# Layer normalization on one core: early rows of the fourth tile on a second queue, and the first tile's statistics in two groups

## Chip, cores, metric

One core of a Trainium2 chip. The metric is the device time of one execution in microseconds (us), smaller is better; executions of this kernel agree within some 0.2%. A profile is one execution recorded by the hardware profiler; its span is 1.6 to 2.0 us shorter than the time of the same execution in the runs here.

## The reference

```python
def setup_inputs():
    batch, seq, dim = 32, 512, 1024
    return {"x": np.random.randn(batch, seq, dim).astype(np.float32), "eps": 1e-5}

def reference(x, eps):
    mean = np.mean(x, axis=-1, keepdims=True)
    var = np.var(x, axis=-1, keepdims=True)
    return ((x - mean) / np.sqrt(var + eps)).astype(np.float32)
```

16384 rows of 1024 floats: 67.1 MB in, 67.1 MB out, and little arithmetic.

## The kernel before

Each of the 128 partitions holds 48 rows of 4 KB, a ring of six tiles of 8 rows. For each tile: a load; `bn_stats` on VectorE (two per row); nine small GpSimd steps that merge the partial statistics; a square root on ScalarE; a reciprocal on VectorE; a product on GpSimd; eight normalising passes on ScalarE, in place; a store. Loads go out on the SyncE queue, stores on the ScalarE queue; the load of tile t waits until tile t-6 is stored.

```python
TILES = (8,) * 15 + (6, 2)
SLOT, SLOTS = 8, 6
HALVES, PARTS = (4, 4), (8,)
# ... first tile: two halves, one on each queue
for n, engine, sem in zip(HALVES, (nc.sync, nc.scalar), (landed[0], later)):
    engine.dma_start(out=ring[:, at+first : at+first+n, :],
                     in_=rows_of(x2, row, K)[:, first : first+n, :]).then_inc(sem, 16)
# ... later tiles, behind the store that frees their place
    dma = nc.sync.dma_start(out=ring[:, at : at+K, :], in_=rows_of(x2, row, K)
                            ).then_inc(landed[t], 16)
    if gone:
        dma._wait_ge(stored[gone[-1]], sixteens(stored, gone[-1]))
# ... VectorE, per tile
    for k in range(K):
        for s in range(NSUB):
            i = nc.vector.bn_stats(...)      # first one waits for the load
    i.then_inc(taken, 1)
    nc.vector.reciprocal(out=rstd[...], in_=std[...])._wait_ge(rooted[t], turn).then_inc(inverse, 1)
# ... GpSimd: nine steps from `taken`, then nmr = -mean * rstd from `inverse`
# ... ScalarE: sqrt, K x activation(Identity, bias=nmr, scale=rstd), then the store
```

## Time and profile before

| | before |
|---|---|
| time, median of 3 runs | 317.88 us (317.74 to 317.92) |
| span of the profile | 315.9 us |
| VectorE, ScalarE, GpSimd busy | 156.8, 153.0, 39.3 us |
| bytes moved, mean rate | 134.24 MB, 425 GB/s |

The engines that compute are idle half the time or more. A packet is what one of the 16 DMA engines moves at a time: a transfer of a whole tile of 8 rows is 128 packets of 32 KB, one for each partition. The row "DMA" of the page gives the share of time for which the 16 DMA engines were busy in each of 40 slices; it and the stretches are shown in the prediction below.

### The profile page before, as it was taken

What the parts mean: (1) busy time and instruction counts of PE and PEld (TensorE: products, weight loads), DVE (VectorE), ACT (ScalarE), POOL (GpSimd) and SP (SyncE); (2) the same over time, 40 slices, a digit from 0 to 9 for tenths busy, and PEclk for the clock granted to TensorE, in tenths of its full rate; (3) what the DMA queues carried; (4) which work ended last, traced back from release to release, by engine and by line L of the source; (5) the groups of instructions that cost most, each with busy time, mean ns of one, the idle gap of its engine ahead of it and who ended that gap; (6) DMA issues with size and microseconds to landing.
All of it is one profiled execution on the core that took longest, in us unless ns stands there. A gap on an engine that the chain in (4) does not pass through costs nothing.

```text
span 315.9 us, 694 instructions
## 1 busy us (share of the span) xinstructions
DVE 156.8 (50%) x274; ACT 153.0 (48%) x146; POOL 39.3 (12%) x174
## 2 busy tenths in 40 slices
DVE  0296595965190752908438093470925619193000
ACT  1006595865925609165190742908338092476600
POOL 0002202022002020020201102011020200203100
DMA  7999999999999999999999999999999999999996
GB/s 292 438 452 411 452 402 407 457 407 461 403 462 415 448 419 444 419 444 431 431 436 427 444 423 440 423 448 415 452 415 456 419 431 442 435 430 427 427 421 288
DMA packets 5043, 134.24 MB, mean 425 GB/s; under 512 B 560, under 2 KB 560, under 8 KB 560
## 3 DMA queue, kind: packets, MB, share of 16 engines
q10 hardware_dynamic: 2592, 69.21, 51.0%
q1 hardware_dynamic: 2448, 65.01, 47.9%
q14 instruction: 3, 0.02, 0.0%
HBM read 67.11 MB, written 67.11 MB: 425 GB/s over the span
## 4 chain that ended last, share of the span: by engine, by line
DMA 61%; DVE 18%; ACT 9%; POOL 4%; issue 2%; ACTq 0%; DVEq 0%; SPq 0%
DMA ring<-in_x_dram 31%; DMA out_dram<-ring 29%; DVE stats L115 17%; ACT ring L210 9%; ACT std L200 1%; POOL dev L173 1%; POOL dev L178 1%; POOL dev L166 0%; POOL dev L171 0%; POOL nmean L162 0%; POOL half L156 0%; POOL half L179 0%; POOL ss L182 0%; DVE rstd L124 0%; POOL nmean L160 0%
## 5 line engine op out<-in xcount | busy, mean ns | idle before, releaser
L115 DVE BATCH_NORM_STATS2 stats<-ring 128x6 f32<-128x512 f32 x256 | 153.5, 678 | 82.2 <-DMA ring<-in_x_dram 81.6
L210 ACT ACTIVATE ring<-ring,nmr,rstd 128x1024 f32<-128x1024 f32 x128 | 146.6, 1227 | 9.3 <-POOL nmr L190 9.3
L200 ACT ACTIVATE std<-ss,eps_t 128x8 f32<-128x8 f32 (+2 forms) x17 | 5.1, 300 | 134.3 <-POOL ss L182 133.9
L156 POOL TENSOR_TENSOR half<-stats 128x16 f32<-128x16 f32 (+2 forms) x17 | 3.9, 232 | 232.9 <-DVE stats L115 232.9
L124 DVE RECIPROCAL rstd<-std 128x8 f32<-128x8 f32 (+2 forms) x17 | 3.4, 200 | 55.4 <-ACT std L200 55.4
L173 POOL TENSOR_SCALAR dev<-dev 128x32 f32<-128x32 f32 (+2 forms) x17 | 5.0, 293 | 1.5
L190 POOL TENSOR_TENSOR nmr<-nmean,rstd 128x8 f32<-128x8 f32 (+2 forms) x17 | 3.5, 203 | 11.9 <-DVE rstd L124 11.9
L178 POOL TENSOR_TENSOR dev<-dev,stats 128x32 f32<-128x32 f32 (+2 forms) x17 | 4.3, 254 | 1.4
L166 POOL TENSOR_TENSOR dev<-stats,nmean 128x32 f32<-128x32 f32 (+2 forms) x17 | 4.1, 239 | 1.4
L171 POOL TENSOR_TENSOR dev<-dev 128x32 f32<-128x32 f32 (+2 forms) x17 | 4.0, 235 | 1.3
L162 POOL TENSOR_SCALAR nmean<-nmean 128x8 f32<-128x8 f32 (+2 forms) x17 | 4.0, 233 | 1.5
L179 POOL TENSOR_TENSOR half<-dev 128x16 f32<-128x16 f32 (+2 forms) x17 | 3.6, 213 | 1.3
L182 POOL TENSOR_TENSOR ss<-half 128x8 f32<-128x8 f32 (+2 forms) x17 | 3.4, 201 | 1.3
L160 POOL TENSOR_TENSOR nmean<-half 128x8 f32<-128x8 f32 (+2 forms) x17 | 3.4, 200 | 1.3
L200 ACT ACT_TABLE_LOAD x1 | 1.3, 1283 | 1.3 <-SPq L52 1.3
L128 DVE MEMSET eps_t<- 128x1 f32 x1 | 0.1, 59 | 1.0 <-SPq L52 1.0
L246 POOL MEMSET const-float32-0.0<- 128x1 f32 x1 | 0.1, 98 | 0.2 <-issue 0.2
L246 POOL MEMSET const-uint8-127<- 128x1 uint8 x1 | 0.1, 102 | 0.0
L246 POOL MEMSET const-bfloat16-1.0<- 128x1 bf16 x1 | 0.1, 101 | 0.0
L246 POOL MEMSET const-float32-1.0<- 128x1 f32 x1 | 0.1, 98 | 0.0
## 6 DMA issues: line engine op xcount, KB each, us to landing
out_dram<-ring ACTq DMA_DIRECT2D x15, 4096.0 KB, 47.4
ring<-in_x_dram SPq DMA_DIRECT2D x14, 4096.0 KB, 44.3
ring<-in_x_dram SPq DMA_DIRECT2D x1, 3072.0 KB, 42.0
out_dram<-ring ACTq DMA_DIRECT2D x1, 3072.0 KB, 17.8
ring<-in_x_dram ACTq DMA_DIRECT2D x1, 2048.0 KB, 12.4
ring<-in_x_dram SPq DMA_DIRECT2D x1, 2048.0 KB, 12.5
ring<-in_x_dram SPq DMA_DIRECT2D x1, 1024.0 KB, 53.7
out_dram<-ring ACTq DMA_DIRECT2D x1, 1024.0 KB, 16.7
```

The lines of the kernel that those rows point to most:

```text
L115: i = nc.vector.bn_stats(out=stats[:, at + k, s, :], in_=ring[:, at + k, s * BN_MAX : (s + 1) * BN_MAX],)
L124: nc.vector.reciprocal(out=rstd[:, at : at + K], in_=std[:, at : at + K])._wait_ge(rooted[t], turn).then_inc(inverse, 1)
L156: g.tensor_tensor(out=h, in0=mean4[:, :, 0:2], in1=mean4[:, :, 2:4], op=ALU.add),
L162: g.tensor_scalar(out=nm, in0=nm, scalar1=-1.0 / H, scalar2=None, op0=ALU.mult),
L166: g.tensor_tensor(out=d, in0=mean4, in1=nm.unsqueeze(2).to_broadcast([P, K, H]), op=ALU.add),
L171: n = gp(g.tensor_mul(out=d, in0=d, in1=d), *n)
L173: g.tensor_scalar(out=d, in0=d, scalar1=float(D // H), scalar2=None, op0=ALU.mult),
L178: n = gp(g.tensor_tensor(out=d, in0=d, in1=m2, op=ALU.add), *n)
L179: n = gp(g.tensor_tensor(out=h, in0=d[:, :, 0:2], in1=d[:, :, 2:4], op=ALU.add), *n)
L190: g.tensor_mul(out=nmr[:, at : at + K], in0=nm, in1=rstd[:, at : at + K]),
L200: nc.scalar.activation(out=std[:, at : at + K], in_=ss[:, at : at + K], func=AF.Sqrt, bias=eps_t[:], scale=1.0 / D,)._wait_ge(*summed[t]). ...
L210: i = nc.scalar.activation(out=ring[:, k, :], in_=ring[:, k, :], func=AF.Identity, bias=nmr[:, k : k + 1], scale=rstd[:, k : k + 1],).then ...
```

## The change

The intent is an earlier start. The first half of tile 0 no longer shares the DMA engines with the second at equal weight, so it lands sooner; each half gets its own chain of statistics, so the first rows are normalised while the second half is still being measured, and the reciprocal of tile 0 becomes a power on GpSimd, so VectorE need not wait for it. Three rows of the fourth tile (index 3) are loaded from the beginning on the ScalarE queue, which has nothing else to do yet. The diff, cut to its core:

```diff
-HALVES, PARTS = (4, 4), (8,)
+HALVES = (4, 4)
+EARLY, AHEAD = 3, 3
+    power = sbuf("power", [P, SLOT])
@@ loads
+    for k in range(AHEAD):
+        load(nc.scalar, EARLY, k, 1, ahead)          # one row each
+        if t == 0:
+            load(nc.sync, t, 0, HALVES[0], landed[t])
+            load(nc.sync, t, HALVES[0], HALVES[1], second)
+            continue
+        first = AHEAD if t == EARLY else 0
+        dma = load(nc.sync, t, first, K - first, landed[t])
@@ VectorE
+        if t == EARLY:
+            nc.vector.wait_ge(ahead, 16 * AHEAD)
+    nc.vector.memset(power[:], -1.0)
+    statistics(0, HALVES[0], landed[0], 16)
+    statistics(HALVES[0], HALVES[1], second, 16)
+    for t in range(1, FIRST):
@@ GpSimd and ScalarE: loops over 18 groups (4, 4, 8, 8, ...) instead of 17 tiles
+        if t:
+            n = inverse, t
+        else:
+            n = gp(g.tensor_tensor(out=rstd[...], in0=std[...], in1=power[:, :K], op=ALU.pow), ...)
```

The store of tile 0 stays one store of 8 rows.

More of the change, by code (lines that the diff above doesn't have):

```diff
@@ L74, in sixteens @@
     def sixteens(sems, t):
-        if sems is stored and t == 0:
-            return 16 * len(PARTS)
         return 16 * sum(1 for s in sems[: t + 1] if s.num == sems[t].num)
@@ L85, in rows_of, with load @@
         return a[row * P : (row + K) * P].rearrange("(p k) d -> p k d", p=P)
-    later = nc.alloc_semaphore("landed_later")
-    K, row, at = plan[0]
-    first = 0
-    for n, engine, sem in zip(HALVES, (nc.sync, nc.scalar), (landed[0], later)):
-        engine.dma_start(
+    groups = []
+    for t, (K, row, at) in enumerate(plan):
+        for n in HALVES if t == 0 else (K,):
+            groups.append((t, at, n))
+            at += n
+    second, ahead = nc.alloc_semaphore("second_half"), nc.alloc_semaphore("ahead")
+    def load(engine, t, first, n, sem):
+        K, row, at = plan[t]
+        return engine.dma_start(
             out=ring[:, at + first : at + first + n, :],
@@ L95 @@
         ).then_inc(sem, 16)
-        first += n
-    assert first == K
-    owner = {r: 0 for r in range(K)}
-    for t, (K, row, at) in list(enumerate(plan))[1:]:
+    for k in range(AHEAD):
+        load(nc.scalar, EARLY, k, 1, ahead)
+    owner = {}
+    for t, (K, row, at) in enumerate(plan):
         gone = sorted({owner[r] for r in range(at, at + K) if r in owner})
@@ L103, with statistics @@
             nc.sync.wait_ge(stored[g], sixteens(stored, g))
-        dma = nc.sync.dma_start(
-            out=ring[:, at : at + K, :], in_=rows_of(x2, row, K)
-        ).then_inc(landed[t], 16)
+        if t == 0:
[4 more added lines that the diff above has]
+        dma = load(nc.sync, t, first, K - first, landed[t])
         if gone:
             dma._wait_ge(stored[gone[-1]], sixteens(stored, gone[-1]))
+    def statistics(at, n, sem, value):
+        for k in range(at, at + n):
+            for s in range(NSUB):
+                i = nc.vector.bn_stats(
+                    out=stats[:, k, s, :],
+                    in_=ring[:, k, s * BN_MAX : (s + 1) * BN_MAX],
+                )
+                if k == at and s == 0:
+                    i._wait_ge(sem, value)
+        i.then_inc(taken, 1)
     def vector(t, arrived, turn):
         K, row, at = plan[t]
-        for k in range(K):
-            for s in range(NSUB):
-                i = nc.vector.bn_stats(
-                    out=stats[:, at + k, s, :],
-                    in_=ring[:, at + k, s * BN_MAX : (s + 1) * BN_MAX],
-                )
-                if k == 0 and s == 0:
-                    i._wait_ge(landed[t], arrived)
-                if t == 0 and k == HALVES[0] and s == 0:
-                    i._wait_ge(later, 16)
-        i.then_inc(taken, 1)
+        if t == EARLY:
+            nc.vector.wait_ge(ahead, 16 * AHEAD)
+        statistics(at, K, landed[t], arrived)
         nc.vector.reciprocal(
@@ L128 @@
     nc.vector.memset(eps_t[:], eps_val)
-    for t in range(FIRST):
+    nc.vector.memset(power[:], -1.0)
+    statistics(0, HALVES[0], landed[0], 16)
+    statistics(HALVES[0], HALVES[1], second, 16)
+    for t in range(1, FIRST):
         vector(t, 16, 1)
@@ L150 @@
     g = nc.gpsimd
-    for t, (K, row, at) in enumerate(plan):
+    for i, (t, at, K) in enumerate(groups):
         parts = stats[:, at : at + K].rearrange("p g s (h c) -> p g (s h) c", h=2)
@@ L157 @@
             taken,
-            t + 1,
+            i + 1,
         )
@@ L187 @@
         )
+        if t:
+            n = inverse, t
+        else:
+            n = gp(
+                g.tensor_tensor(
+                    out=rstd[:, at : at + K],
+                    in0=std[:, at : at + K],
+                    in1=power[:, :K],
+                    op=ALU.pow,
+                ),
+                rooted[t],
+                i + 1,
+            )
         ready.append(
@@ L192 @@
                 ),
-                inverse,
-                t + 1,
+                *n,
             )
         )
-    for t, (K, row, at) in enumerate(plan):
+    for i, (t, at, n) in enumerate(groups):
         nc.scalar.activation(
-            out=std[:, at : at + K],
-            in_=ss[:, at : at + K],
+            out=std[:, at : at + n],
+            in_=ss[:, at : at + n],
             func=AF.Sqrt,
@@ L205 @@
             scale=1.0 / D,
-        )._wait_ge(*summed[t]).then_inc(rooted[t], 1)
-        parts = PARTS if t == 0 else (K,)
-        ends = [sum(parts[: i + 1]) for i in range(len(parts))]
-        for k in range(at, at + K):
-            i = nc.scalar.activation(
+        )._wait_ge(*summed[i]).then_inc(rooted[t], 1)
+        for k in range(at, at + n):
+            a = nc.scalar.activation(
                 out=ring[:, k, :],
@@ L217 @@
             if k == at:
-                i._wait_ge(*ready[t])
-            if k - at + 1 in ends:
-                n = parts[ends.index(k - at + 1)]
-                a = k + 1 - n
-                nc.scalar.dma_start(
-                    out=rows_of(o2, row, K)[:, a - at : a - at + n, :], in_=ring[:, a : a + n, :]
-                )._wait_ge(act, row + k - at + 1).then_inc(stored[t], 16)
+                a._wait_ge(*ready[i])
+        K, row, at = plan[t]
+        if k == at + K - 1:
+            nc.scalar.dma_start(
+                out=rows_of(o2, row, K), in_=ring[:, at : at + K, :]
+            )._wait_ge(act, row + K).then_inc(stored[t], 16)
     for t in range(len(plan)):
```

## The prediction

> **What bounds the kernel now.** I read the views in this order: the page's slices, its DMA queues, the busy time by stretches, the timeline of the first 80 us, and the packet records behind the trace. Arithmetic is idle half of the time (VectorE 156.8 us, ScalarE 153.0 us of 315.9), the transfers never are:
>
> ```profile
> DMA  7999999999999999999999999999999999999996
> DMA packets 5043, 134.24 MB, mean 425 GB/s; under 512 B 560, under 2 KB 560, under 8 KB 560
> q10 hardware_dynamic: 2592, 69.21, 51.0%
> q1 hardware_dynamic: 2448, 65.01, 47.9%
> HBM read 67.11 MB, written 67.11 MB: 425 GB/s over the span
> ```
>
> Only the first and last of the 40 slices are below 9 tenths, and the two queues together take 98.9% of the time of all 16 engines. The bytes are the least possible: x is read once and the output written once. The stretches say the same (columns: the stretch in us, its length, busy us of VectorE, ScalarE and GpSimd with counts, TensorE clock, DMA share, GB/s):
>
> ```profile
> 0.00:4.00 4.00, 0.06 (x1) 1.28 (x1) 0.19 (x4) 1.00 0.53 143
> 4.00:36.00 32.00, 19.25 (x33) 9.46 (x9) 2.32 (x10) 1.00 1.02 441
> 36.00:40.00 4.00, 0.83 (x3) 0.61 (x2) 2.32 (x10) 1.00 1.06 393
> 40.00:280.00 240.00, 129.96 (x226) 129.66 (x124) 30.18 (x130) 1.00 1.00 432
> 280.00:300.00 20.00, 6.66 (x13) 12.03 (x12) 4.32 (x20) 1.00 1.01 433
> 300.00:313.00 13.00, 0.00 (x0) 0.00 (x0) 0.00 (x0) 1.00 0.97 417
> 313.00:315.90 2.90, 0.00 (x0) 0.00 (x0) 0.00 (x0) 1.00 0.18 73
> ```
>
> Loads alone (4 to 36), loads with stores (40 to 280) and stores alone (300 to 313) all run at about the same rate, so it makes no difference to the total which of them the engines do at a moment, as long as they do one.
>
> The view of the chain that ended last could mislead here: it gives 61% to DMA and 18% to VectorE statistics. Its early part does run through VectorE, but the DMA engines were full of later tiles' loads all that while. What the change speeds up is this start:
>
> ```profile
> 13.48 9.59 DVE L115 BATCH_NORM_STATS2 stats<-ring 128x6 f32<-128x512 f32 x16 [12.42 <-DMA ring<-in_x_dram]
> 26.81 9.16 ACT L210 ACTIVATE ring<-ring,nmr,rstd 128x1024 f32<-128x1024 f32 x8 [0.55 <-POOL nmr L190]
> 36.00 0.35 ACTq L222 DMA_DIRECT2D out_dram<-ring  x1
> 298.01 0.34 ACTq L222 DMA_DIRECT2D out_dram<-ring  x1
> ```
>
> The first store is issued at 36.0 us, the last at 298.0, and the last data lands near 314. The store queue therefore still holds some 15 us of work when the last piece of arithmetic is over: the compute path has that much room at the end.
>
> **The packet records** (the trace holds start, size and duration of every packet; no view prints them singly). The median packet takes 309 ns for 8 KB, 611 ns for 16 KB, 912 ns for 24 KB, 1213 ns for 32 KB: about 602 ns per 16 KB and 8 or 9 ns for the packet. One engine's share is 232 packets of 32 KB, 16 of 24 KB, 16 of 16 KB and 16 of 8 KB: 281.4 + 14.6 + 9.8 + 4.9 = 310.7 us. Before it lie 1.9 us to the first packet; the first packet of each engine took about 1290 ns instead of 611 (0.7 us of exposed latency); and around 39 us, as the first store's packets begin, one load packet of each engine took about 1.8 us instead of 1.21 (0.6 us, the 393 GB/s above). Sum 313.9; some 2 us remain for the last completion, the unequal ends of the engines and the final waits, which makes the span of 315.9. The 317.88 us of the unprofiled runs are 2 us more. There is nothing larger than 1 us in this sum that an earlier start of arithmetic could remove.
>
> **What the Trainium skill says.** "DMA: Bandwidth & Descriptors", section "Where 436 GB/s comes from", puts the ceiling of the 16 engines at 435 GB/s; the trace agrees, with 432 over 240 us. The same page, section "Queues, rings and completion order", has each engine alternate between queues packet by packet, whatever their size. The trace agrees: in the mixed stretch packets of both queues are 32 KB and alternate, and a store of 4 MB takes 43 us from issue, mostly queued, with 19.4 us between tiles. This matters for the change: a 4 KB packet on one queue is answered by a 16 or 32 KB one on the other. The section "Issuing engines are not separate DMA queues" says that issuing from several engines saves only issue time (here 0.37 to 0.39 us per issue). "HBM Reference", "Specifications (TRN2)", puts a lone core at about 425 GB/s; the page's mean is 425.
>
> **The change, part by part.**
>
> *Loads.* Removed: the second half of tile 0 from the ScalarE queue. It now follows the first on the SyncE queue, while ScalarE issues three loads of one row (512 KB each, 128 packets of 4 KB); the fourth tile's own load shrinks to five rows (20 KB packets). Bytes are unchanged. Per engine there are 24 more packets, at about 9 ns: 0.2 us; three more completions of 9 ns are nothing. An estimate from the fit: a 4 KB packet takes 0.16 us. A pair of 16 KB and 4 KB is then 0.77 us, a pair of 32 KB and 4 KB 1.37 us. From the first packet at 1.9 us, with 0.9 us for the first latencies, eight pairs bring half one at about 9.5 (before, 13.48), eight more bring half two at 15.7, and eight with tile 1's packets bring tile 1 and the early rows together at 26.7. Tile 1 thus lands when VectorE used to begin on it (26.41).
>
> *Statistics in two groups.* Eight statistics take 4.8 us (half of 9.6): 9.5 to 14.3. The nine GpSimd steps took 2.8 us (23.15 to 25.93), and cost nearly the same for 4 rows as for 8, since they are 0.20 to 0.30 us each: 17.2. Square root 0.3, then a power on GpSimd in place of VectorE's reciprocal (no duration in this trace; as an estimate 0.2 to 0.5), product 0.2: ScalarE begins about 18.1 and ends four rows at 22.7. Group two: 15.7 to 20.5, sum at 23.4, rows 24.3 to 28.9. Extra work is nine GpSimd steps, a product, two powers and one square root, some 4 us, on engines at 12% and 48%. Gain: VectorE is no longer held for 3.2 us by tile 0's reciprocal, and the first store is issued at about 29 instead of 36.
>
> *What 7 us earlier is worth.* From 29 to 36 the engines now carry stores on half their packets, where they carried only loads. About 7 x 0.216 = 1.5 MB moves from the end to the beginning, and as much loading moves later. The load stream ends about 3.5 us later (the last load landed at 288.75), the last store is issued at about 301.5, and the queue then holds 12 us of stores instead of 15. The end does not move. Sum: +0.2 us for small packets, 0 for the earlier store.
>
> *The fourth tile.* With stores beginning at 29, tile 2 lands near 39.6 and tile 3, five rows at about 2.0 us a pair, near 55. VectorE wants tile 3 at about 53. Whole, it would land near 59. The early rows repair a wait that the earlier store makes, but the wait stands beside full DMA.
>
> **Rivals.**
> 1. *The start is on the path, and 7 us (2.2%) come off.* For it: the chain view runs through VectorE and GpSimd from 13.48 to 75 us. Against it: DMA share 1.02 from 4 to 36 us; a chain of waits does not say that the engines were idle. It would give 311, below the 313.9 that the packets need.
> 2. *Half of it, 3.5 us,* if only-store time at the end ran slower than mixed time. The 417 GB/s from 300 to 313 hints at it; but store packets there take 1214 ns against 1213 in the middle, so that is the uneven count of packets at the edge. It would give about 314.5.
> 3. *A new starvation.* The ring holds six tiles; with less loaded ahead, the store queue could run dry in the steady state or at the end. My times have store 0's packets end near 52 and store 1 issued at 49 (the first store's packets came 3.8 us after its issue), so a short dry spell is likely. Loads fill it, so it costs only what a restart of stores costs, up to the 0.6 us seen at 39. At the end store 15 would be issued about 6 us before its predecessors are drained. A real loss needs both queues empty: two more us would give 320.
> 4. *A better ramp:* a 4 KB first packet might hide the first latency. At most 0.7 us: 317.2.
>
> **Range and chances.** 317.88 + 0.2 for packets, and a few hundredths for a possible restart: 318.1. Rival 4 sets the low end, the restart and unlucky ends of the engines the high end: 317.4 to 318.9. Two per cent are 6.4 us; faster by that is excluded by the packet sum, slower needs a starvation that the room of 6 to 12 us speaks against.
>
> **What would show it.** First statistics near 9.5, first store near 29, VectorE's wait for the reciprocal of tile 0 gone, 384 more packets under 8 KB, DMA share 9 tenths in the same 38 slices, last store issued near 301 instead of 298, same end. I am wrong if a stretch between 4 and 313 us shows a rate below 425 GB/s for 20 us, or if the power or the small loads delay the first store beyond 36 us.

## The result, and the profile after

| | before | after |
|---|---|---|
| time, median | 317.87 us (317.74 to 317.92, 4 runs) | 318.42 us (318.31 to 318.82, 4 runs) |
| span of the profile | 315.9 us | 316.7 us |
| first store issued | 36.00 us | 29.64 us |
| last store issued | 298.01 us | 305.72 us |
| last data written (packet records) | 314.24 us | 314.42 us |

The ratio is 1.002 (95% interval 1.0003 to 1.0038): the same within 2%, and a little slower. A ratio here and below is the mean time of one kernel's fast runs over that of the other's of the same rounds, so it is not quite the ratio of the medians quoted.

The page of the changed kernel, its slices and queues:

```profile
DMA  7999999999999999999999999999999999999996
DMA packets 5476, 134.25 MB, mean 424 GB/s; under 512 B 608, under 2 KB 608, under 8 KB 992
q10 hardware_dynamic: 2880, 68.68, 50.4%
q1 hardware_dynamic: 2592, 65.54, 48.5%
```

The same 38 slices are full. The 384 data packets of 4 KB appear under 8 KB (992 less the 608 small ones). Selected lines of the timeline (start, length, engine, line, what, and in brackets the idle time before it with its releaser):

```profile
9.44 4.84 DVE L128 BATCH_NORM_STATS2 stats<-ring 128x6 f32<-128x512 f32 x8 [8.33 <-DMA ring<-in_x_dram]
15.63 4.85 DVE L128 BATCH_NORM_STATS2 stats<-ring 128x6 f32<-128x512 f32 x8 [1.35 <-DMA ring<-in_x_dram]
17.37 1.04 POOL L212 TENSOR_TENSOR rstd<-std,power 128x4 f32<-128x4 f32 x1 [0.41 <-ACT std L232]
26.60 9.59 DVE L128 BATCH_NORM_STATS2 stats<-ring 128x6 f32<-128x512 f32 x16 [6.12 <-DMA ring<-in_x_dram]
29.64 0.35 ACTq L251 DMA_DIRECT2D out_dram<-ring  x1
54.39 9.59 DVE L128 BATCH_NORM_STATS2 stats<-ring 128x6 f32<-128x512 f32 x16 [0.93 <-DMA ring<-in_x_dram]
...
305.72 0.34 ACTq L251 DMA_DIRECT2D out_dram<-ring  x1
```

Everything the change was made for happened: statistics 4 us earlier, the store 6.4 us earlier. And the stretches, in the columns of the prediction:

```profile
4.00:36.00 32.00, 19.09 (x32) 9.75 (x10) 6.39 (x22) 1.00 1.02 424
36.00:40.00 4.00, 0.39 (x2) 0.35 (x2) 2.35 (x10) 1.00 1.01 434
40.00:280.00 240.00, 127.13 (x220) 122.77 (x117) 30.13 (x129) 1.00 1.00 433
300.00:313.00 13.00, 0.17 (x1) 4.77 (x5) 1.33 (x7) 1.00 0.97 417
313.00:316.70 3.70, 0.00 (x0) 0.00 (x0) 0.00 (x0) 1.00 0.23 95
```

The share is 1.0 as before. The 424 of the first line holds what lay at 36 to 40 us before (393 GB/s there): the stall as stores begin (load packets that take longer than usual while the first stores start), now at 31 to 36 us. ScalarE and GpSimd now still work after 300 us, where they had finished: the end of the arithmetic has moved closer to the end of the transfers.

The profiled span grew by 0.73 us. By the packet records, 0.18 us of it lies before the last data is written. The other 0.55 us come after it, in the closing handshake of the engines.

### The profile page after: what moved, and what is told of

The parts are those of the page before. It is cut to its first block, busy times and chain, and to the rows that moved or that the text cites. A ratio compares the mean times of both kernels' runs of the same rounds, so it can differ in the third digit from the quotient of the medians.

```text
span 316.7 us, 712 instructions
## 1 busy us (share of the span) xinstructions
DVE 157.0 (50%) x274; ACT 153.3 (48%) x147; POOL 43.6 (14%) x186
## 4 chain that ended last, share of the span: by engine, by line
DVE 43%; another core or an unknown queue 23%; DMA 12%; POOL 10%; ACT 4%; issue 4%; SPq 0%; ACTq 0%; DVEq 0%
DVE stats L128 42%; DMA ring<-in_x_dram 12%; ACT ring L240 3%; ACT std L232 1%; POOL dev L193 1%; POOL dev L198 1%; POOL dev L186 1%; POOL nmean L182 1%; POOL dev L191 1%; POOL half L176 1%; POOL half L199 1%; POOL nmean L180 1%; POOL ss L202 1%; DVE rstd L141 1%
## 5 line engine op out<-in xcount | busy, mean ns | idle before, releaser
L240 ACT ACTIVATE ring<-ring,nmr,rstd 128x1024 f32<-128x1024 f32 x128 | 146.8, 1226 | 11.7 <-POOL nmr L223 11.7
L232 ACT ACTIVATE std<-ss,eps_t 128x8 f32<-128x8 f32 (+3 forms) x18 | 5.4, 299 | 138.4 <-POOL ss L202 138.0
L176 POOL TENSOR_TENSOR half<-stats 128x16 f32<-128x16 f32 (+3 forms) x18 | 4.1, 230 | 235.4 <-DVE stats L128 235.4
L193 POOL TENSOR_SCALAR dev<-dev 128x32 f32<-128x32 f32 (+3 forms) x18 | 5.1, 281 | 1.6
L223 POOL TENSOR_TENSOR nmr<-nmean,rstd 128x8 f32<-128x8 f32 (+3 forms) x18 | 3.7, 205 | 11.4 <-DVE rstd L141 11.3
L198 POOL TENSOR_TENSOR dev<-dev,stats 128x32 f32<-128x32 f32 (+3 forms) x18 | 4.5, 252 | 1.5
L182 POOL TENSOR_SCALAR nmean<-nmean 128x8 f32<-128x8 f32 (+3 forms) x18 | 4.3, 238 | 1.6
L186 POOL TENSOR_TENSOR dev<-stats,nmean 128x32 f32<-128x32 f32 (+3 forms) x18 | 4.3, 238 | 1.5
L191 POOL TENSOR_TENSOR dev<-dev 128x32 f32<-128x32 f32 (+3 forms) x18 | 4.2, 235 | 1.4
L199 POOL TENSOR_TENSOR half<-dev 128x16 f32<-128x16 f32 (+3 forms) x18 | 3.8, 213 | 1.4
L180 POOL TENSOR_TENSOR nmean<-half 128x8 f32<-128x8 f32 (+3 forms) x18 | 3.6, 203 | 1.4
```

The lines of the kernel that those rows point to most:

```text
L176: g.tensor_tensor(out=h, in0=mean4[:, :, 0:2], in1=mean4[:, :, 2:4], op=ALU.add),
L180: n = gp(g.tensor_tensor(out=nm, in0=h[:, :, 0], in1=h[:, :, 1], op=ALU.add), *n)
L182: g.tensor_scalar(out=nm, in0=nm, scalar1=-1.0 / H, scalar2=None, op0=ALU.mult),
L186: g.tensor_tensor(out=d, in0=mean4, in1=nm.unsqueeze(2).to_broadcast([P, K, H]), op=ALU.add),
L191: n = gp(g.tensor_mul(out=d, in0=d, in1=d), *n)
L193: g.tensor_scalar(out=d, in0=d, scalar1=float(D // H), scalar2=None, op0=ALU.mult),
```

## The experiments

The theory to test: the time is the bytes and packets of 16 always busy DMA engines, plus a fixed beginning and end, so that neither start nor end of the arithmetic counts while there is room. Rival: the start is on the path, as the chain view has it. Each kernel was compared with the kernel before on the same chip (before: 317.84 to 317.89 us), and all results were correct.

**late_1: the start made 9.6 us later.** The kernel before with extra statistics, whose results go nowhere:

```diff
+        if t == 0:
+            nc.vector.wait_ge(landed[0], 16)
+            nc.vector.wait_ge(later, 16)
+            for j in range(16):
+                nc.vector.bn_stats(out=extra[:, j, :], in_=ring[...])
```

> The kernel before with 16 more statistics (9.6 us of VectorE, results unused) ahead of tile 0's own: first store at about 45.6 us instead of 36.0. Theory (always full DMA engines; loads of later tiles fill the time, the ring of six tiles is full only near 60 us): 317.9 +- 0.5. Rival (the start of the arithmetic is on the path, as the chain view suggests): 327.

Measured: first store at 45.51 us, time 318.50 us (318.18 to 319.02), ratio 1.0019. A start 9.5 us later costs 0.6 us, 0.1 more than the range I had given. In its profile the last data comes 0.54 us later than before (314.78); packets account for 0.1 of this, and the rest is that the engines end less evenly. The start is not on the path; the rival falls.

**late_4: the start made 38 us later.** The same edit with 64 statistics.

> The same with 64 more statistics (38.4 us): first store at about 74.4 us, its data from about 76. Theory: the six tiles of the ring are loaded by about 60 us, then both queues are empty until the first store; 15 to 18 us are lost: 332 to 337, and the slices near 60 to 75 us show DMA shares near 0. Rival (path): 356. If it stays near 318, the ring is not what bounds the loads.

Measured: first store at 74.16 us, time 334.50 us, ratio 1.0519. Now the slices show a hole (page, then one stretch):

```profile
DMA  7999999309899999999999999999999999999997
```

```profile
64.00:72.00 8.00, 7.55 (x14) 7.33 (x8) 0.29 (x2) 1.00 0.00 0
```

The sixth load's data is in at 62.1 us, the first store's packets begin at 75.0 us (packet records), and in all 15 us per engine are empty. So the start has room until about 60 us, where the ring is full; the kernel before uses 36 of it. Making it 29.6 adds room at a place that had enough.

**before_tail and after_tail: the end made later.** Five extra copies of one row, ahead of the normalisation of the tile of 6 rows, in either kernel:

```diff
+        if t == 15:
+            nc.scalar.wait_ge(*ready[t])
+            for j in range(5):
+                d = nc.scalar.activation(out=ring[:, at, :], in_=ring[:, at, :],
+                                         func=AF.Identity).then_inc(spare, 1)
+                if j:
+                    d._wait_ge(spare, j)
+            nc.scalar.wait_ge(spare, 5)
```

> The kernel before with five more copies of one row on ScalarE (about 6.5 us) between the statistics and the normalisation of the tile of 6 rows near the end: its store is issued at about 301 instead of 294.4. Theory: the store ahead of it drains until 304.5, so the room of some 9 us less 1 to 2 us of issue covers it: 317.9 +- 0.5. Rival (the end of the arithmetic sets the time): 324.

> The same five copies in the changed kernel: its store goes from 302.1 to about 308.7. Theory (the earlier first store has used up the room at the end; store 14 drains at 304.7): the DMA engines are empty from 304.7 to about 310, 4.5 to 6 us are lost: 323 to 324.5. Rival (the room is 12 us, as my prediction had it): 318.4.

Measured: before_tail 318.10 us (ratio 1.0006), its store of 6 rows issued at 300.40 instead of 294.43; after_tail 321.85 us (321.07 to 322.73; ratio 1.0129), its store issued at 306.35. One stretch of each, first before_tail:

```profile
304.00:308.00 4.00, 0.00 (x0) 0.00 (x0) 0.00 (x0) 1.00 1.00 430
```

and after_tail:

```profile
304.00:308.00 4.00, 0.17 (x1) 3.08 (x5) 0.20 (x1) 1.00 0.25 107
```

The same delay is free in the kernel before and leaves the DMA engines empty for 3.0 of these 4 us in the changed one. I had expected 4.5 to 6 us; the direction is right, the size too large, partly because in this profile the tile itself arrived 1.3 us earlier than in that of the changed kernel. What was shown: the earlier start is paid for with room at the end.

**groups_only: the statistics in two groups, without early rows.**

```diff
-EARLY, AHEAD = 3, 3
+EARLY, AHEAD = -1, 0
-            load(nc.sync, t, HALVES[0], HALVES[1], second)
+            load(nc.scalar, t, HALVES[0], HALVES[1], second)
```

> Tile 0's statistics in two groups, its second half on the ScalarE queue as before, no early rows. Theory (the 16 DMA engines are always full, so only the packets, the stalls and the closing count): 280 packets per engine as before, last store data at 314.2 +- 0.3 us of the span, first store near 33 us, time 317.7 to 318.3, the difference to before coming from the closing after the last data. Rival (the start is on the path): first store 3 us earlier gives about 315.

Measured: 318.06 us (317.89 to 318.23), ratio 1.0006 (0.9993 to 1.0019); first store at 33.71; last data at 314.27, as in the kernel before. As the theory had it. The closing, from the last data to the end of the span, is 2.03 us instead of 1.69; the profiled execution took only 0.16 us more (317.91 against 317.75).

**ahead_only: early rows without the two groups.**

```diff
-        for n in HALVES if t == 0 else (K,):
+        for n in (K,):
+                if sem is landed[0] and k == HALVES[0] and s == 0:
+                    i._wait_ge(second, 16)
-    statistics(0, HALVES[0], landed[0], 16)
-    statistics(HALVES[0], HALVES[1], second, 16)
-    for t in range(1, FIRST):
+    for t in range(FIRST):
```

(and tile 0 uses VectorE's reciprocal again)

> Early rows and the halves one behind the other on the SyncE queue, but tile 0's statistics in one group with VectorE's reciprocal. Theory: 24 more packets per engine at 9 ns, so last data at 314.4 +- 0.3 us, time 317.9 to 318.5; first store near 33 us. Rival (small packets on the second queue are what costs the 0.55 us): 318.4 as the full change, with all of the difference before the last data.

Measured: 323.05 us (321.02 to 323.86), ratio 1.0154. Neither expectation: 4.6 us slower than the full change, with the same bytes and the same packets. Its stretch from 60 to 280 us, all in the mixed state:

```profile
60.00:280.00 220.00, 110.66 (x192) 106.19 (x101) 25.77 (x111) 1.00 1.00 430
```

The same stretch of the changed kernel:

```profile
60.00:280.00 220.00, 111.72 (x194) 107.15 (x103) 27.79 (x119) 1.00 1.00 433
```

The engines are as full as ever, and move less: 430 against 433 GB/s. In the packet records the 32 KB packets of this stretch take 1223 ns on average instead of 1213.4, 6% of them over 1.02 times the median (0.1% in the kernel before) and up to 2162. The last data comes 5.0 us later than in the changed kernel (319.41). Longer packets are 1.8 us of this (314.40 us busy per engine against 312.59). The other 3.2 us are idle time near the end: from 304 to 308 us the engines are empty for 0.7 us each on average, and the rest is that they end unevenly. I take it that tiles land when their slowest engine is done and that the room at the end was small; this was not tested. So there is a cost that I had not thought of: the same packets can take longer.

**early_as_one: the three early rows in one load.**

```diff
-    for k in range(AHEAD):
-        load(nc.scalar, EARLY, k, 1, ahead)
+    load(nc.scalar, EARLY, 0, AHEAD, ahead)
-            nc.vector.wait_ge(ahead, 16 * AHEAD)
+            nc.vector.wait_ge(ahead, 16)
```

> The full change, but the three early rows in one load: 8 packets of 12 KB per engine in place of 24 of 4 KB. Theory: 16 packets fewer, 0.14 us less before the last data than the full change, 318.1 to 318.5 in all; the early rows are done by about 11 us and the first half lands about 1.5 us later. Rival (loading one by one matters for the time): over 319 or under 317.5.

Measured: 319.50 us (318.89 to 320.07), ratio 1.0054. It is 1 us over the theory's range and, by its letter, inside the rival's (over 319); four of five runs are over 319. The loading one by one may thus matter, though why is not shown. First statistics at 11.80 us, first store at 32.02. The profiled run was the fastest of the five (318.89), with a stall of 1.2 us per engine as the stores begin, against 0.9 in the changed kernel, and last data at 314.88. The rest of the median's gap is in runs without a profile and stays open.

**after_pad: 64 small fills at the start of VectorE's program.**

```diff
+    for j in range(64):
+        nc.vector.memset(pad[:, j : j + 1], 0.0)
```

> The full change with 64 tiny fills (59 ns each) at the start of VectorE's program, where it waits for data anyway. Theory (0.5 us of the loss is a fetch of instructions that falls into the closing handshake after the last data): transfers end where they did (314.4), and the stretch from the last data to the end changes from 2.2 us to about 1.7, or at least moves by 0.3 us or more. Rival (the loss is in the transfers): closing stays at 1.7 to 2.2 in whatever way and the last data lands over 0.4 us later than in the kernel before.

Measured: 318.99 to 334.70 us in 8 runs. Only two count as fast, 318.99 and 322.57 (ratio 1.0251); the others, the profiled one (323.87) too, count as slow because they lie over 1.5% above the fastest of this kernel, although the clock stays 1.0. The closing did not move as expected: 2.08 us, near the changed kernel's 2.24. By its letter the rival came true, since the last data is late too (320.01), but only in a profile that counts as slow. I draw nothing from the sizes; that so small an edit can spread the runs by 16 us made me look at the packets.

**dephase_8 and dephase_16: are the engines out of step?** After the eight experiments above (late_1 to after_pad) I supposed that packets are fast while the 16 engines read together and write together, and slow when some read while others write. Each engine takes load and store packets in turn (2.43 us a pair); an extra short packet on half of the engines should shift them against the rest. The kernel before with four small loads behind tile 5, of 8 or of 16 partitions:

```diff
+        if t == SLOTS:
+            for j in range(4):
+                nc.sync.dma_start(out=spare[8 * j : 8 * (j + 1), :],    # 16 in dephase_16
+                    in_=x2[0 : 2 * 8].rearrange("(p k) d -> p (k d)", k=2),
+                ).then_inc(shifted, 16)
```

> The kernel before with four extra loads of 8 partitions x 8 KB (results unused) on the load queue behind tile 5, in the mixed stretch: one packet of 309 ns on each of 8 engines and none on the others, each followed by a store packet of 1213 ns. Four pairs take 6.09 us, 1.24 us (half a period of 2.43) off the step of the rest, so from some 84 us on 8 engines should read while the other 8 write. Phase theory: packets slow down by 1 to 10 per cent from there on, time 321 to 331. Rival (phase does not matter): the extra 1.24 us on 8 engines, 319.1.

> Control of the one before: the same four loads with 16 partitions, one packet on each of the 16 engines, so that all shift alike and stay in step. Both theories: 4 x 0.31 = 1.24 us longer than the kernel before, 319.1 +- 0.5. If it is 321 or more, the extra loads themselves do harm, not the phase.

Measured: dephase_8 323.31 us (322.68 to 324.06), ratio 1.0165; dephase_16 319.97 us (319.70 to 320.51), ratio 1.0067. The loads of 8 partitions move half the bytes and cost 3.3 us more. The stretch of both, first dephase_8:

```profile
60.00:280.00 220.00, 106.80 (x186) 105.66 (x101) 25.54 (x110) 1.00 1.00 427
```

then dephase_16:

```profile
60.00:280.00 220.00, 110.14 (x192) 105.77 (x101) 26.41 (x113) 1.00 1.00 432
```

In the packet records, the 32 KB packets of this stretch take 1230 ns on average in dephase_8 (up to 2159) and 1214 in dephase_16. dephase_16 itself is 0.4 us over its range; its engines were busy 1.5 us longer than before instead of 1.24, and ended more unevenly. In dephase_8 the packets from 60 to 84 us, ahead of the extra loads, still take 1214 ns; from 96 us on, behind them, 1226 on average, against 1213 in dephase_16. So extra packets on half of the engines slow the packets after them, and extra packets on all hardly do. That this is the shift is inferred: six of the eight packets of the second extra load begin 2.73 us after one of the first, as they would on the same eight engines, and four times 2.73 us is 4.5 pairs, half a pair out of step. My wording of it, "half read while half write", does not hold: in before_tail 7 to 11 of the 16 engines are reading in 45% of the moments from 60 to 280 us, and its packets are all fast. Which engines must not be out of step with which stays open; the records do not name a packet's engine.

**after_again: the changed kernel once more, beside the last three.**

> The changed kernel itself again, as a control on the chip of this call. Theory formed after the first eight runs (a packet takes 1213 ns while all 16 engines read at the same time and write at the same time, and 1250 to 1600 ns while about half of them read and half write; the start of the stores sets the phase): 318.3 to 319 with runs spread by under 1 us if it falls into step each time; some runs above 320 if it is chance. Rival (the pad and the ungrouped statistics have costs of their own): 318.3 to 318.8 without exception.

Measured: 318.55 us (318.43 to 318.74), ratio 1.0021 (1.0008 to 1.0035). The nine runs lie within 0.5 us: the times are steady, and both profiles have fast packets (1213.4 and 1213.5 ns on average). The theory and the rival both allow this, so the run does not decide between them. Why the changed kernel stays fast and ahead_only does not was not found out.

**twelve_rows: larger tiles, to beat both.**

```diff
-TILES = (8,) * 15 + (6, 2)
-SLOT, SLOTS = 8, 6
-FIRST, TURNS = 3, 2
-HALVES, PARTS = (4, 4), (8,)
+TILES = (12,) * 10 + (6, 2)
+SLOT, SLOTS = 12, 4
+FIRST, TURNS = 2, 2
+HALVES, PARTS = (6, 6), (12,)
```

> The kernel before with tiles of 12 rows (ring of 4 tiles, first tile in halves of 6): 200 data packets per engine in place of 280, of 48 KB. Theory (9 ns for each packet): 0.7 us less, 317.2, if the engines stay in step; first store near 48 us, still inside the ring's room of about 60. Rival (room is too small with 4 slots): the end or the ring starves, 320 or more.

Measured: 318.65 us (317.98 to 319.62), ratio 1.0015. The engines were busy 312.20 us instead of 312.28, so the saved packets were nearly eaten up by a longer stall as stores begin (1.2 us per engine against 0.65), and one engine ended alone, at 316.4 us, with most others done by 314.5 (this was the slowest of its runs). No version beat the kernel before.

## Why the prediction was right

The time was inside the range (318.42 against 318.1, range 317.4 to 318.9), and for the reason given: the late_ kernels show that the start has room until the ring is full, and the tail pair that the end has room until the queue of stores is drained. Step by step:

- *Loads and start.* 9.5, 15.7, 26.7 us expected; 9.44, 15.63, 26.60 measured. Adding up packets in turn, 16 and 4 KB or 32 and 4 KB, was good to 0.1 us. The sums as written give 9.0, 15.1 and 26.1, though: the time from the last packet to the first statistic (0.58 us for the first half, 8.86 to 9.44) is in the results and not in the text. Tile 3 was waited for by 0.93 us, expected 2.
- *First store.* 29 expected, 29.64 measured. The power on GpSimd took 1.04 us; my estimate without any record was 0.2 to 0.5.
- *Cost of packets.* 0.2 us expected. The last data came 0.18 us later in the first profile, 0.27 in the second (314.51). It is about the sum of three: 24 packets at 9 ns (0.22), the stall as the stores begin (0.90 us per engine instead of 0.65), and first packets faster in sum by 0.2 (they took 1319 ns before, not the 1290 of the prediction, and 1103 after). The prediction had the first term alone; that the other two nearly cancel is luck.
- *The mis-sized term.* I wrote that some 2 us remain at the end and left them alone. They did not stay: from the last data to the end of the span 1.69 us before, 2.24 and 2.13 after. This, not the transfers, is most of the difference. The end of the two kernels by line, first before:

```profile
L229 POOLq EVENT_SEMAPHORE  x3: 42/43/43, 305.0 to 314.7; - x3
```

```profile
L52 POOLq COMPARE_BRANCH  x1: 33/33/33, 314.8 to 314.8; - x1
```

```profile
L260 DVEq DRAIN  x2: 10/14/19, 295.4 to 315.4; - x2
L260 DVEq EVENT_SEMAPHORE  x2: 21/21/21, 315.3 to 315.9; - x2
```

then after (the second time in a line is the start of the last one):

```profile
L258 POOLq EVENT_SEMAPHORE  x3: 43/43/43, 305.2 to 314.9; - x3
```

```profile
L56 POOLq COMPARE_BRANCH  x1: 33/33/33, 315.3 to 315.3; - x1
```

```profile
L289 DVEq DRAIN  x2: 19/65/111, 303.2 to 316.3; - x2
L289 DVEq EVENT_SEMAPHORE  x2: 21/21/21, 315.8 to 316.6; - x2
```

GpSimd's branch out of its last wait comes 0.4 us after it instead of 0.1, and VectorE's drain 0.5 us after its first handshake instead of 0.1. Over all 14 traces the first goes with the kernels of 18 groups and the second with those that wait for early rows, without exception; closings are 1.4 to 1.7 us in the kernel before and its variants, 1.8 in ahead_only, 2.0 in groups_only, 2.1 to 2.2 in the others. In all the kernels of 18 groups an instruction fetch of 8 KB lies 1.4 to 1.6 us after the last data, inside the handshake; elsewhere it comes 2.1 us after it or later, behind the handshake. The Trainium skill ("Runtime: NRT & Kernel Launch", section "Instruction fetch mechanics") says that a taken branch whose target is not at hand must wait for a fetch. The fetch does not bear this out: its packet starts some 0.7 us after GpSimd's branch has run (1.58 and 0.90 us after the last data), and ahead_only has VectorE's late drain while its fetch comes behind the handshake. The kernel meant to move the fetch did not move it either. So the cause stays open; that the time lies there is shown.

- *The end.* Here the working was wrong, without harm to the time. I let the loads end 3.5 us later and the last store go out at 301.5 us; they ended 7.7 us later (last load data at 294.85 instead of 287.18), and the store went out at 305.72. I divided the displaced 1.5 MB by the full rate, although in the mixed stretch loads have half of it: that alone gives 7. From the records, as an estimate: store packets begin 6.1 us earlier; the eight pairs of a 20 KB load and a 32 KB store give loads less than half, 3.6 us more (8 x (1.213 - 0.761)); a dry spell of the store queue of 2.3 us (50.50 to 52.78, foreseen under rival 3) gives some back. 6.1 + 3.6 - 2.3 = 7.4. The count agrees: ahead of the last load data, 112.8 store packets per engine are sent instead of 106.8, and store packets take 7.4 us more. The other 0.3 us are the small packets and the stall. So the queue held 8.7 us of stores when the last one was issued, not 12, and the room before the store of 6 rows is about 1 us instead of the 6 that I claimed, as after_tail shows.
- *The criterion.* By its letter the 424 GB/s from 4 to 36 us would have made me wrong ("below 425 GB/s for 20 us"). It was badly set: a stall that had lain just behind this stretch moved into it. Such a test must cover the same events in both kernels.
- *Rivals.* 1 and 2 fell with late_1; of 3 the dry spell came, and packets around its end took at most 0.05 us per engine longer; 4 was there, 0.2 us.

What I did not foresee is that equal packets may take longer, by 0.8% on average in ahead_only and 1.4% in dephase_8. It did not touch this change, which is luck as well: with the uneven ends that came with it, it made ahead_only 4.6 us slower than the change that contains it, and would have made the prediction wrong had the change been that half.

## What to carry to other kernels

Where the DMA engines are full from first to last, sum up bytes and packets first: an earlier start then only exchanges room at one end for room at the other, and what remains are parts of a microsecond in the beginning, the change from loads to stores, and the closing. Measure the room by delaying start and end on purpose, before spending work to shorten them. And when time moves with the same bytes at full DMA share, look at how long single packets take.

## What the Trainium skill lacked or had wrong

- "DMA: Bandwidth & Descriptors", "Queues, rings and completion order": that each engine alternates packets was right, and gave landing times to 0.1 us. Lacking: packets of the same size can take longer at a DMA share of 1.0 (after extra packets on half of the engines 1230 ns, on all 1214 ns on average, 3.3 us in the time).
- Same page, "Latency and other measured facts": about 600 ns to the first byte on this path. From the issue's start it was 1.0 us at the beginning and 0.85 us for the first store of late_4, with idle engines; behind a busy load queue the first store's packets came 3.8 us (before) and 4.1 us (after) after the issue. The page has no figure for a first packet behind a busy queue, nor for the stall of 0.6 to 1.2 us per engine as stores begin.
- "GPSIMD Engine Reference", section "Performance versus the Vector engine": no figure for a power; it took 1.04 us for 128x4, five times an addition of that size (0.20 us).
- "Runtime: NRT & Kernel Launch", "Instruction fetch mechanics": has the mechanism of fetches, but not that the end of a kernel can differ by 0.5 us (1.69 and 2.24 us after the last data) between two programs that do the same work.
